# A two-stream transformer layer on one Trainium2 core: the stage between two feed-forward groups rearranged

## The chip, the cores and the metric

The kernel runs on one NeuronCore of a Trainium2 chip. The metric is the device time of one execution in microseconds, lower is better, taken as the median of several runs. The engines, each with its own instruction queue that is worked off in order, are TensorE (PE, matrix products into the banks of PSUM), VectorE (DVE), ScalarE (ACT), GpSimd (POOL) and SyncE (SP, which here issues the DMAs).

## The reference

One encoder layer with the same weights is applied to two request groups: 1024 frames of a new stream and 32 frames of a running one, so 1056 columns in all, with 1024 features and everything in float32.

```python
mod = silu(c) @ w_ada + b_ada
sh1, sc1, g1, sh2, sc2, g2 = split(mod)
h = x * (1 + sc1) + sh1
...                                   # one input projection; three mixers: mLSTM, forgetting attention, gMLP
mix = concat([hm, hf, hg]) @ w_o
x = layer_norm(ALPHA * x + (1 + g1) * mix, ln1_g, ln1_b)
h = x * (1 + sc2) + sh2
y = (silu(h @ w_gate) * (h @ w_up)) @ w_down      # 1024 -> 2816 -> 1024
x = layer_norm(ALPHA * x + (1 + g2) * y, ln2_g, ln2_b)
```

## The kernel before

Features lie on the 128 partitions (KT = 8 tiles of 128 features), columns along the free axis. The 1056 columns are worked as two streams: stream 0 has 512 columns in two cuts of 256, stream 1 has 544 columns in two cuts of 272 (of which the last 32 are the running stream, with its own modulation, so that a cut's work on columns is split into 240 + 32 there). A float32 product is made of three products of rounded halves: `weights` loads a weight tile (`raw`, on SP), rounds it on ACT (`whi`, L102) and takes the rest on DVE (`wlo`, L103); `gemm` issues for each k three matmuls (L114, L115, L116). An activation is split in the same way into a rounded half `ah` and a rest `al`.

The order of the work is this. Input projection and stream 0's mixers; output projection `wo(0)`, norm `ln1(0)`; then the feed-forward part of stream 0 in six groups of its 22 hidden tiles (3, 3, 4, 4, 4, 4), woven by a scheduler with the mixers of stream 1. A group is its `up` calls (gate and up product of one hidden tile, silu by three activations on ACT, L977 to L979, then L980, L981 and L983 on DVE) and a `down` (eight output tiles m, for two cuts each; `sublayer_end` adds a down's result to the residual `z` on DVE, L918, which frees the PSUM bank). The first up of a group is issued before the downs of the group ahead of it.

Before the last group (`g == WOB`, the sixth) stream 1's output projection stands: `wo_mix(1)` reads the mixers' result back from DRAM (16 loads through a tag `tmp` of four buffers, each rounded on ACT, L884, and split on DVE, L885), `wo_res(1)` loads the residual into `z`, `wo(1)` multiplies by w_o, and `ln1(1)` normalises. Then come the last group's ups and downs, and after them the feed-forward part of stream 1.

The norm subtracts a pivot first so that sums of squares keep their precision: `ln_pivot` takes a mean over the first tile (a matmul by `ones8`, L833), copies it (`pv`, ACT, L834) and subtracts it from that tile (L835); for every other tile POOL subtracts it (L915) ahead of the eviction L918. `ln_sum` collects sums (POOL, L845) and squares (ACT L844, DVE L847). `ln_stats` makes the factors r and e of the norm from them (two matmuls, then ACT and DVE, L854 to L866). `ln1` then does for each tile: times r (DVE, L931), plus e (L932, every fourth on POOL), gain and bias (POOL, L935), the rounded half (ACT, L937) and the rest (DVE, L938). `ln1_res` prepares the residual (L947). For stream 0 the pivot that its second norm (`ln2`) needs is subtracted in the downs of the last group.

PSUM has a pool `pg` of three banks, which gate and up products, downs and wo share; a pool `pu` of three further banks for the up products is opened only for stream 1's feed-forward part.

The order of the instructions is set by the Tile framework's scheduler, which places them on each engine by an estimate of the times; `issue_after(x)` holds what is issued in its block behind the instruction x. In the trace a tile carries the name of the phase in which it was made (`wo`, `lna` for the first norm, `up`, `dn`), and z of stream 0 is called `mlstm_z`.

## Time and profile before

| | us |
|---|---|
| median of three runs | 1460.4 (1458.1 to 1462.01) |
| profiled execution, own time | 1461.59 |
| its span, first to last instruction | 1459.8 |
| PE busy | 1396.7 |
| DVE busy | 964.8 |
| ACT busy | 627.2 |
| POOL busy | 283.8 |

The profile is one execution. Its span is the time between the first and the last instruction; 1.8 us lie around it. An engine counts as busy while it executes; "granted clock" is the share of its full clock at which TensorE was allowed to run. A row of a group of instructions names line, engine, operation, written tile and read tiles (buffer numbers left out), shapes and count, then the busy time, the mean duration of one in ns, and the idle time ahead of them with what ended most of it.

### The profile page before, as it was taken

The page shows a single profiled execution, that of the slowest core. Times are in us where ns is not written, and L with a number is a line of the kernel's source. Part 1 is how long each engine was busy: PE and PEld are TensorE (multiplying, and loading weights), DVE is VectorE, ACT ScalarE, POOL GpSimd, SP SyncE. Part 2 cuts the span into 40 slices and gives each one's busy share as a digit, 9 for nine tenths or more (in the row PEclk, how much of TensorE's full clock was granted, in tenths as well). Part 3 has the DMA queues.
Part 4 walks back from the last instruction along what each step waited for, and adds up shares of the span by engine and source line. Part 5 has one row for each costly group of instructions (what it writes and reads, how often), then busy time and mean ns, then how long its engine had stood idle before and what let it go on. Part 6 is the DMA issues. An engine that isn't in the chain of part 4 may idle for free.

```text
span 1459.8 us, 28886 instructions
## 1 busy us (share of the span) xinstructions
PE 1396.7 (96%) x11141; PEld 1345.1 (92%) x11141; DVE 964.8 (66%) x2220; ACT 627.2 (43%) x1365; POOL 283.8 (19%) x335
## 2 busy tenths in 40 slices
PE   7999999999999899999999998998999999999995
PEld 4899988989898799999999998998999999999994
DVE  5558655678698677787877755677648545454676
ACT  3223244534453454555454542334445342424353
POOL 0104100143187300000000000647601000000433
PEclk9999999999999999999999998999999999999997
DMA  9754768563754755444433535321224322222331
GB/s 361 260 194 126 221 199 243 194 197 121 250 188 144 204 166 151 126 125 139 130 111 108 101 94 136 109 86 59 87 73 137 110 87 87 88 88 87 124 108 62
DMA packets 120865, 207.33 MB, mean 142 GB/s; under 512 B 21380, under 2 KB 76300, under 8 KB 120728
## 3 DMA queue, kind: packets, MB, share of 16 engines
q1 hardware_dynamic: 120728, 205.49, 44.8%
q8 instruction: 88, 1.44, 0.4%
q14 instruction: 49, 0.40, 0.1%
HBM read 173.78 MB, written 31.66 MB: 141 GB/s over the span
## 4 chain that ended last, share of the span: by engine, by line
PE 80%; DMA 6%; DVE 6%; POOL 3%; issue 2%; ACT 1%; SPq 1%; DVEq 0%; ACTq 0%; POOLq 0%
PE up_g L115 7%; PE up_g L116 7%; PE up_g L114 7%; PE dn_g L114 4%; PE dn_g L115 4%; PE dn_g L116 4%; PE up_u L116 3%; PE up_u L115 3%; PE up_u L114 3%; PE tm_g L279 3%; PE tm_g L280 3%; PE tm_g L281 3%; PE fox_t L729 2%; PE wo_g L116 2%; PE wo_g L115 2%
## 5 line engine op out<-in xcount | busy, mean ns | idle before, releaser
L114 PE MATMUL up_g<-wo_ah,up_whi 128*128 128x256 f32 (+1 forms) x1056 | 304.1, 289 | 13.2 <-DVE up_sil L980 5.6
L115 PE MATMUL up_g<-wo_al,up_whi 128*128 128x256 f32 (+1 forms) x1056 | 305.3, 289 | 0.1
L116 PE MATMUL up_g<-wo_ah,up_wlo 128*128 128x256 f32 (+1 forms) x1056 | 304.6, 289 | 0.0
L114 PEld LDWEIGHTS up_g<-wo_ah,up_whi 128*128 128x128 f32 x1056 | 201.9, 191 | 16.5 <-DVE up_sil L980 6.0
L115 PEld LDWEIGHTS up_g<-wo_al,up_whi 128*128 128x128 f32 x1056 | 202.1, 191 | 1.4 <-DVE wo_al L938 0.7
L116 PEld LDWEIGHTS up_g<-wo_ah,up_wlo 128*128 128x128 f32 x1056 | 201.7, 191 | 0.7 <-DVE up_wlo L103 0.4
L103 DVE TENSOR_TENSOR up_wlo<-up_raw,up_whi 128x1024 fp32r<-128x1024 f32 x94 | 120.8, 1285 | 68.5 <-ACT up_whi L102 68.2
L102 ACT CAST up_whi<-up_raw 128x1024 fp32r<-128x1024 f32 x94 | 98.5, 1048 | 142.3 <-PE dn_u L115 53.9
L114 PE MATMUL dn_g<-up_acth,dn_whi 128*128 128x256 f32 (+1 forms) x496 | 146.7, 296 | 9.5 <-DVE mlstm_z L918 6.4
L115 PE MATMUL dn_g<-up_actl,dn_whi 128*128 128x256 f32 (+1 forms) x496 | 144.4, 291 | 0.0
L116 PE MATMUL dn_g<-up_acth,dn_wlo 128*128 128x256 f32 (+1 forms) x496 | 143.8, 290 | 0.0
L280 PE MATMUL tm_g<-tm_wlo,start_h1h 128*128 128x256 f32 (+1 forms) x384 | 110.8, 289 | 0.0
L281 PE MATMUL tm_g<-tm_whi,start_h1l 128*128 128x256 f32 (+1 forms) x384 | 110.4, 288 | 0.0
L279 PE MATMUL tm_g<-tm_whi,start_h1h 128*128 128x256 f32 (+1 forms) x384 | 109.8, 287 | 0.2 <-ACT tm_mixs L630 0.2
L114 PE MATMUL fm_g<-start_h1h,fm_whi 128*128 128x256 f32 (+2 forms) x344 | 102.0, 302 | 6.1 <-DVE fm_qkl L364 2.2
L114 PEld LDWEIGHTS dn_g<-up_acth,dn_whi 128*128 128x128 f32 x496 | 96.7, 195 | 11.5 <-DVE mlstm_z L918 7.5
L115 PE MATMUL fm_g<-start_h1l,fm_whi 128*128 128x256 f32 (+2 forms) x344 | 101.8, 296 | 0.2 <-DVE start_h1l L220 0.2
L116 PE MATMUL up_u<-wo_ah,up_wlo 128*128 128x272 f32 x352 | 101.9, 290 | 0.0
L114 PE MATMUL up_u<-wo_ah,up_whi 128*128 128x272 f32 x352 | 101.2, 288 | 0.0
L115 PE MATMUL up_u<-wo_al,up_whi 128*128 128x272 f32 x352 | 101.0, 287 | 0.0
L116 PE MATMUL fm_g<-start_h1h,fm_wlo 128*128 128x256 f32 (+2 forms) x344 | 100.8, 294 | 0.0
L115 PEld LDWEIGHTS dn_g<-up_actl,dn_whi 128*128 128x128 f32 x496 | 96.9, 195 | 0.3
(458 smaller groups left out, 3758.9 us busy)
## 6 DMA issues: line engine op xcount, KB each, us to landing
up_raw<-w_gu SPq DMA_DIRECT2D x94, 512.0 KB
dn_raw<-w_dn SPq DMA_DIRECT2D x30, 512.0 KB
ada_late<-w_ada SPq DMA_DIRECT2D x24, 512.0 KB
wo_raw<-w_o SPq DMA_DIRECT2D x24, 512.0 KB
ada_araw<-w_ada SPq DMA_DIRECT2D x16, 512.0 KB
fm_raw<-w_in_f SPq DMA_DIRECT2D x16, 512.0 KB
tm_raw<-w_in SPq DMA_DIRECT2D x12, 512.0 KB
dn_raw<-w_dn SPq DMA_DIRECT2D x16, 384.0 KB
```

The costliest lines, as they stand in the source:

```text
L102: nc.scalar.copy(hi[:, :w], raw[:, :w])
L103: (eng or nc.vector).tensor_tensor(lo[:, :w], raw[:, :w], f(hi[:, :w]), ALU.subtract)
L114: nc.tensor.matmul(ps, hi, xh(k), start=start and k == 0, stop=False)
L115: nc.tensor.matmul(ps, hi, xl(k), start=False, stop=False)
L116: nc.tensor.matmul(ps, lo, xh(k), start=False, stop=stop and k == n - 1)
L279: nc.tensor.matmul(ps[:, :ncol], xh, hi, start=k == 0, stop=False)
L280: nc.tensor.matmul(ps[:, :ncol], xh, lo, start=False, stop=False)
L281: nc.tensor.matmul(ps[:, :ncol], xl, hi, start=False, stop=k == 7)
L729: nc.tensor.transpose(ps[:, y * P:(y + 1) * P], probs[y][:, b * P:(b + 1) * P], self.ident)
```

## The change

Five things are done. (a) Stream 0's pivot is taken and subtracted in the downs of the fifth group (`g == WOB - 1`) instead of the last group's; the last downs only collect the sums. (b) In `ln1`, for both streams, gain and bias move from POOL to ACT (an activation `Identity` with scale and bias columns). (c) The pool `pu` is opened ahead of stream 1's output projection, so that the last group's ups use six banks. (d) The last group's second up, `up(0, 19)`, is issued ahead of the mix, the mix is issued behind the last residual addition of the fifth group's downs (`lastz`), and each residual tile of stream 1 is loaded inside `wo`. (e) The other two ups are woven with the norm of stream 1 (`up` and `ln1` become generators), and `ln1_res(1)` comes after the last downs.

```diff
-    def wo(self, c, st, cuts, eng):
+    def wo(self, c, st, cuts, eng, res=None):
...
+        if res:
+            self.z[c] = self.t(res, [P, KT, GN[c]], F32, f"z{c}", 1)
+        z = self.z[c]
         ko = self.KORDER
         for m in range(KT):
+            if res:
+                self.load(z[:, m], self.d["xT"][m, :, GO[c]:GO[c] + GN[c]])
             w = self.weights(self.d["w_o"][m], KT, P, eng)
...
         for x, y, i in self.parts(c, a, b):
-            self.nc.vector.scalar_tensor_tensor(z[:, m, x:y], ps[:, x - a:y - a], g[i], z[:, m, x:y],
-                                                ALU.mult, ALU.add)
+            self.lastz = self.nc.vector.scalar_tensor_tensor(z[:, m, x:y], ps[:, x - a:y - a], g[i], z[:, m, x:y],
+                                                             ALU.mult, ALU.add)
...
         for k in range(KT):
+            yield
+            self.phase = f"lna{c}"
             zk = z[:, k, sl]
...
             for x, y, i in self.parts(c, a, b):
-                nc.gpsimd.tensor_scalar(h[:, x - a:y - a], z[:, k, x:y], self.lng[:, k, i:i + 1],
-                                        self.lnb[:, k, i:i + 1], ALU.mult, ALU.add)
+                nc.scalar.activation(h[:, x - a:y - a], z[:, k, x:y], AF.Identity, bias=self.lnb[:, k, i:i + 1],
+                                     scale=self.lng[:, k, i:i + 1])
...
             if g == WOB:
                 s4.close()
                 s3.close()
+                self.pu, self.utag = self.pool("pu", 3, space=PSUM), "gu"
                 pb = self.pb = self.pool("pb", side="right")
+                weave(self.up(0, j0 + 1, act, pa, MM[0]))
                 self.operand(1, pb)
-                self.wo_mix(1, self.KORDER)
-                self.wo_res(1, pb)
+                with tc.issue_after(self.lastz.ins):
+                    self.wo_mix(1, self.KORDER)
                 stb = self.ln_begin(nc.gpsimd)
-                self.wo(1, stb, MM[1], nc.vector)
+                self.wo(1, stb, MM[1], nc.vector, pb)
                 self.operand(1, pb)
-                for a, b in MM[1]:
-                    self.ln1(1, stb, a, b)
+
+                def norm():
+                    for a, b in MM[1]:
+                        yield from self.ln1(1, stb, a, b)
+
+                def fill():
+                    for j in range(j0 + 2, j0 + nj):
+                        yield from self.up(0, j, act, pa, MM[0])
+
+                weave(fill(), norm())
+                continue
...
-            if g == WOB:
-                self.ln1_res(1)
-            if g < last:
+            if g == WOB - 1:
+                st = self.ln_begin(nc.gpsimd, sum=False)
+                self.down(0, g, act, MM[0], st)
+            else:
                 self.down(0, g, act, MM[0])
-        st = self.ln_begin(nc.gpsimd)
+        st.update(pivot=False, sum=True)
         self.down(0, last, act, MM[0], st)
+        self.ln1_res(1)
         s5.close()
         pa = self.pool("pa1")
-        self.pu, self.utag = self.pool("pu", 3, space=PSUM), "gu"
```

What the scheduler makes of it is seen in three places. In the changed kernel line numbers are a few higher: the eviction L918 is L923, the pivot's subtraction L915 is L920, the norm's L931, L932, L935, L937, L938 are L938, L939, L942, L944, L945, the silu's L980, L981, L983 are L990, L991, L993, and `ln1_res`'s L947 is L954.

The first place is DVE at the end of the fifth group's downs, first before (`dn_g` is a down's bank, `wo_tmp` a loaded piece of the mix):

```order
L918 SCALAR_TENSOR_TENSOR mlstm_z_837_4328<-dn_g_12260,start_mod_136,mlstm_z_837_4328 128x256
L885 TENSOR_TENSOR dn_al_2300_12406<-wo_tmp_12408,dn_ah_2298_12404 128x272
L885 TENSOR_TENSOR dn_al_2300_12406<-wo_tmp_12412,dn_ah_2298_12404 128x272
L885 TENSOR_TENSOR dn_al_2300_12406<-wo_tmp_12416,dn_ah_2298_12404 128x272
L885 TENSOR_TENSOR dn_al_2300_12406<-wo_tmp_12420,dn_ah_2298_12404 128x272
L918 SCALAR_TENSOR_TENSOR mlstm_z_837_4328<-dn_g_12280,start_mod_136,mlstm_z_837_4328 128x256
L103 TENSOR_TENSOR wo_wlo_12487<-wo_raw_12484,wo_whi_12486 128x1024
L918 SCALAR_TENSOR_TENSOR mlstm_z_837_4328<-dn_g_12294,start_mod_136,mlstm_z_837_4328 128x256
L918 SCALAR_TENSOR_TENSOR mlstm_z_837_4328<-dn_g_12308,start_mod_136,mlstm_z_837_4328 128x256
L885 TENSOR_TENSOR dn_al_2300_12406<-wo_tmp_12424,dn_ah_2298_12404 128x272
```

The splits L885 of the mix stand between the evictions L918. On the same engine in the changed kernel, from the last eviction of these downs on:

```order
L923 SCALAR_TENSOR_TENSOR mlstm_z_837_4328<-dn_g_12408,start_mod_136,mlstm_z_837_4328 128x256
L885 TENSOR_TENSOR up_al_2319_12564<-wo_tmp_12566,up_ah_2317_12562 128x272
L885 TENSOR_TENSOR up_al_2319_12564<-wo_tmp_12570,up_ah_2317_12562 128x272
L885 TENSOR_TENSOR up_al_2319_12564<-wo_tmp_12574,up_ah_2317_12562 128x272
L885 TENSOR_TENSOR up_al_2319_12564<-wo_tmp_12578,up_ah_2317_12562 128x272
L103 TENSOR_TENSOR wo_wlo_12638<-wo_raw_12635,wo_whi_12637 128x1024
L885 TENSOR_TENSOR up_al_2319_12564<-wo_tmp_12582,up_ah_2317_12562 128x272
L885 TENSOR_TENSOR up_al_2319_12564<-wo_tmp_12586,up_ah_2317_12562 128x272
L885 TENSOR_TENSOR up_al_2319_12564<-wo_tmp_12590,up_ah_2317_12562 128x272
L885 TENSOR_TENSOR up_al_2319_12564<-wo_tmp_12594,up_ah_2317_12562 128x272
L990 TENSOR_TENSOR up_sil_12496<-up_g_12446,up_sil_12496 128x256
```

All sixteen splits now follow the last eviction, and the first silu product of up(0,19), L990, stands behind eight of them, its second (not shown) behind fourteen. The same downs now begin with the pivot: DVE has L835 for both cuts there, and POOL the row below, ahead of the pivot subtractions of stream 1 that stood first before:

```order
L761 MEMSET foxs_q_1826_8499 128x192
L920 TENSOR_TENSOR mlstm_z_837_4328<-mlstm_z_837_4328,up_pv_12152 128x256 x14
L920 TENSOR_TENSOR wo_z_2340_12633<-wo_z_2340_12633,wo_pv_12632 128x272 x7
L845 TENSOR_TENSOR wo_zs_12630<-wo_z_2340_12633 128x272
L920 TENSOR_TENSOR wo_z_2340_12633<-wo_z_2340_12633,wo_pv_12632 128x272 x7
```

The fourteen subtractions of stream 0 do the seven tiles of the first cut, then the seven of the second.

The second place is DVE in `ln1(0)`, at the statistics of the second cut; L364 frees a bank that q/k projections (`fm_g`) hold. Before:

```order
L863 SCALAR_TENSOR_TENSOR lna_tmp_6019<-lna_tmp_6019,wo_pv_5357 128x256
L864 TENSOR_TENSOR lna_tmp_6019<-lna_tmp_6019,wo_pv_5357 128x256
L865 SCALAR_TENSOR_TENSOR wo_pv_5357<-lna_tmp_6019,wo_pv_5357 128x256
L103 TENSOR_TENSOR up_wlo_8707<-up_raw_8704,up_whi_8706 128x1024
L364 SCALAR_TENSOR_TENSOR fm_qkl_6292<-fm_g_6266,start_qsc_127,fm_qkh_6291 128x272
L866 SCALAR_TENSOR_TENSOR wo_qs_5356<-lna_t_6015,wo_pv_5357 128x256
L931 TENSOR_TENSOR mlstm_z_837_4328<-mlstm_z_837_4328,wo_pv_5357 128x256 x8
L364 SCALAR_TENSOR_TENSOR fm_qkl_6333<-fm_g_6307,start_qsc_127,fm_qkh_6332 128x272
```

And in the changed kernel:

```order
L103 TENSOR_TENSOR up_wlo_8707<-up_raw_8704,up_whi_8706 128x1024
L364 SCALAR_TENSOR_TENSOR fm_qkl_6292<-fm_g_6266,start_qsc_127,fm_qkh_6291 128x272
L863 SCALAR_TENSOR_TENSOR lna_tmp_6019<-lna_tmp_6019,wo_pv_5357 128x256
L864 TENSOR_TENSOR lna_tmp_6019<-lna_tmp_6019,wo_pv_5357 128x256
L364 SCALAR_TENSOR_TENSOR fm_qkl_6333<-fm_g_6307,start_qsc_127,fm_qkh_6332 128x272
L865 SCALAR_TENSOR_TENSOR wo_pv_5357<-lna_tmp_6019,wo_pv_5357 128x256
L866 SCALAR_TENSOR_TENSOR wo_qs_5356<-lna_t_6015,wo_pv_5357 128x256
L938 TENSOR_TENSOR mlstm_z_837_4328<-mlstm_z_837_4328,wo_pv_5357 128x256 x8
```

Two of the L364 have moved ahead of the statistics and of the eight products by r.

The third place is DVE in the second half of `ln1(1)`. Before, this half stood ahead of the last downs, with the ups' L980 between its rows:

```order
L938 TENSOR_TENSOR wo_al_2381_13039<-lna_tmp_13123,wo_ah_2379_13037 128x272
L981 TENSOR_TENSOR up_sil_13422<-up_g_13397,up_sil_13422 128x256
L980 TENSOR_TENSOR up_sil_13494<-up_g_13444,up_sil_13494 128x256
L938 TENSOR_TENSOR wo_al_2381_13039<-lna_tmp_13130,wo_ah_2379_13037 128x272
L938 TENSOR_TENSOR wo_al_2381_13039<-lna_tmp_13137,wo_ah_2379_13037 128x272
L981 TENSOR_TENSOR up_sil_13494<-up_g_13469,up_sil_13494 128x256
```

And in the changed kernel, where the last downs have begun (`dn_g` and `dn_u` are their banks, of both pools):

```order
L938 TENSOR_TENSOR wo_z_2340_12633<-wo_z_2340_12633,wo_pv_12632 128x272 x8
L923 SCALAR_TENSOR_TENSOR mlstm_z_837_4328<-dn_g_13666,start_mod_136,mlstm_z_837_4328 128x256
L939 TENSOR_TENSOR wo_z_2340_12633<-wo_z_2340_12633,wo_qs_12631 128x272
L923 SCALAR_TENSOR_TENSOR mlstm_z_837_4328<-dn_g_13609,start_mod_136,mlstm_z_837_4328 128x256
L939 TENSOR_TENSOR wo_z_2340_12633<-wo_z_2340_12633,wo_qs_12631 128x272
L923 SCALAR_TENSOR_TENSOR mlstm_z_837_4328<-dn_u_13642,start_mod_136,mlstm_z_837_4328 128x256
L939 TENSOR_TENSOR wo_z_2340_12633<-wo_z_2340_12633,wo_qs_12631 128x272
```

The half's rows now stand between the evictions L923 of the last downs; its L945 follow later, the first behind ten of the sixteen evictions.

More of the change, by code (lines that the diff above doesn't have):

```diff
@@ L890, in wo_res @@
             self.load(z[:, k], self.d["xT"][k, :, GO[c]:GO[c] + GN[c]])
-    def wo(self, c, st, cuts, eng):
+    def wo(self, c, st, cuts, eng, res=None):
         self.phase = f"wo{c}"
-        nc, z, hh, hl = self.nc, self.z[c], self.hh[c], self.hl[c]
+        nc, hh, hl = self.nc, self.hh[c], self.hl[c]
+        if res:
+            self.z[c] = self.t(res, [P, KT, GN[c]], F32, f"z{c}", 1)
+        z = self.z[c]
         ko = self.KORDER
         for m in range(KT):
+            if res:
+                self.load(z[:, m], self.d["xT"][m, :, GO[c]:GO[c] + GN[c]])
             w = self.weights(self.d["w_o"][m], KT, P, eng)
@@ L975, in up @@
                 ps.append(p)
+                if i == 0:
+                    yield
+                    self.phase = f"up{c}"
             s = self.t(self.p2, [P, 272], F32, "sil", 4)[:, :b - a]
@@ L983, in up @@
             nc.vector.tensor_tensor(al[:, a:b], s, f(ah[:, a:b]), ALU.subtract)
+            yield
+            self.phase = f"up{c}"
     def last_weights(self, dst, units):
@@ L1168, in run @@
         for a, b in MM[0]:
-            self.ln1(0, st, a, b)
+            weave(self.ln1(0, st, a, b))
         for h in range(PRE, 8):
@@ L1186, in run @@
                 s3.close()
+                self.pu, self.utag = self.pool("pu", 3, space=PSUM), "gu"
                 pb = self.pb = self.pool("pb", side="right")
+                weave(self.up(0, j0 + 1, act, pa, MM[0]))
                 self.operand(1, pb)
-                self.wo_mix(1, self.KORDER)
-                self.wo_res(1, pb)
+                with tc.issue_after(self.lastz.ins):
+                    self.wo_mix(1, self.KORDER)
                 stb = self.ln_begin(nc.gpsimd)
-                self.wo(1, stb, MM[1], nc.vector)
+                self.wo(1, stb, MM[1], nc.vector, pb)
                 self.operand(1, pb)
-                for a, b in MM[1]:
-                    self.ln1(1, stb, a, b)
+                def norm():
[6 more added lines that the diff above has]
+                continue
             for j in range(j0 + (g > 0), j0 + nj + (g < last)):
-                self.up(0, j, act, pa, MM[0])
+                weave(self.up(0, j, act, pa, MM[0]))
                 if j < 4:
                     self.ada(20 + j, self.wp, "raw", RAW, self.pg, "g")
-            if g == WOB:
-                self.ln1_res(1)
-            if g < last:
+            if g == WOB - 1:
+                st = self.ln_begin(nc.gpsimd, sum=False)
+                self.down(0, g, act, MM[0], st)
+            else:
                 self.down(0, g, act, MM[0])
-        st = self.ln_begin(nc.gpsimd)
+        st.update(pivot=False, sum=True)
         self.down(0, last, act, MM[0], st)
+        self.ln1_res(1)
         s5.close()
         pa = self.pool("pa1")
-        self.pu, self.utag = self.pool("pu", 3, space=PSUM), "gu"
         act = {}
@@ L1211, in run @@
             for j in range(j0 + (g > 0), j0 + nj + 1):
-                self.up(1, j, act, pa, MM[1])
+                weave(self.up(1, j, act, pa, MM[1]))
             if g == 0:
@@ L1226, in run @@
             for j in range(j0 + 1 + (half and UPF), j0 + nj):
-                self.up(1, j, (act, act2)[half], pa, ((a, b),))
+                weave(self.up(1, j, (act, act2)[half], pa, ((a, b),)))
             if half == 0:
@@ L1230, in run @@
                 for j in range(j0 + 1, j0 + 1 + UPF):
-                    self.up(1, j, act2, pa, (LN[1][1],))
+                    weave(self.up(1, j, act2, pa, (LN[1][1],)))
                 w.update(self.last_weights(((h[:, :n], l[:, :n]), (h[:, n:2 * n], l[:, n:2 * n])), (0, 1)))
```

## Prediction

> **What bounds the kernel now.** I read the page's busy shares first, then its chain, then a table of TensorE (PE) by stage, and last the waits of PE in the stages that showed a loss.
>
> ```profile
> PE 1396.7 (96%) x11141; PEld 1345.1 (92%) x11141; DVE 964.8 (66%) x2220; ACT 627.2 (43%) x1365; POOL 283.8 (19%) x335
> PE 80%; DMA 6%; DVE 6%; POOL 3%; issue 2%; ACT 1%; SPq 1%; DVEq 0%; ACTq 0%; POOLq 0%
> ```
>
> PE is busy for 96% of the span and is 80% of the chain, and the change keeps its matmuls. So the change can only move time in which PE stands still or runs at a lowered clock. Where that is, the stages tell (columns: start and end, length, PE busy and instructions, granted clock, DMA share, GB/s):
>
> ```profile
> 464.00:506.00 42.00, 33.72 (x248) 0.94 0.71 185
> 506.00:850.00 344.00, 343.36 (x2821) 1.00 0.45 129
> 850.00:903.00 53.00, 52.51 (x444) 0.94 0.35 87
> 903.00:914.00 11.00, 6.54 (x33) 0.69 0.93 304
> 914.00:962.00 48.00, 48.00 (x382) 1.00 0.29 102
> 962.00:1033.00 71.00, 60.35 (x445) 0.93 0.19 61
> 1065.00:1460.00 395.00, 377.61 (x2986) 0.98 0.29 97
> ```
>
> Three stages that the change touches lose time. I count for each the idle time plus the part of its length that the clock took. The first norm (464 to 506) loses 8.3 + 42 x 0.06 = 10.8 us. The end of the fifth group's downs (903 to 914) loses 4.5 + 11 x 0.31 = 7.9 us. The second norm with its ups and the pivot (962 to 1033) loses 10.65 + 71 x 0.07 = 15.6 us. Together that is 34 us, the most that these edits can return. The full stages also give the price of a matmul: 343/2821 = 0.122 us for 256 columns, 48/382 = 0.126 us for 272.
>
> The waits of PE in the three, first norm, fifth group, second norm (columns: waited for, us in total, times, longest):
>
> ```profile
> PE up_g L114 <- DVE fm_qkl L364: 4.0, 3, 2.1
> PE up_g L114 <- ACT up_whi L102: 2.9, 1, 2.9
> PE up_g L114 <- ACT wo_ah L937: 0.8, 1, 0.8
> ...
> PE dn_g L114 <- DVE mlstm_z L918: 6.4, 4, 4.5
> ...
> PE up_g L114 <- DVE up_sil L980: 5.6, 2, 2.9
> PE dn_g L114 <- DVE up_sil L980: 3.0, 1, 3.0
> PE dn_g L114 <- DVE mlstm_z L918: 1.9, 3, 0.9
> ```
>
> All are waits for a PSUM bank or a weight whose eviction or split stands in DVE's queue, in order, behind something late. In the second norm that is L938, which waits for ACT, which waits for POOL's affine:
>
> ```profile
> ACT wo_ah L937 <- POOL lna_tmp L935: 18.5, 12, 4.5
> ...
> DVE wo_al L938 <- ACT wo_ah L937: 8.6, 9, 2.0
> ```
>
> **The change, part by part.**
>
> *Affine on ACT (both norms).* One tile needs these operations:
>
> ```profile
> L935 POOL TENSOR_SCALAR lna_tmp<-mlstm_z,wo_lng,wo_lnb 128x256 f32<-128x256 f32 x16 | 14.5, 914 | 0.7 <-DVE mlstm_z L932 0.7
> L1024 ACT ACTIVATE mlstm_z<-mlstm_z,start_colp x16: 585/595/604, 1095.1 to 1120.1; 128x256 f32<-128x256 f32 x16
> L937 ACT CAST wo_ah<-lna_tmp 128x272 fp32r<-128x272 f32 x16 | 6.7, 416 | 18.5 <-POOL lna_tmp L935 18.5
> L931 DVE TENSOR_TENSOR wo_z<-wo_z,wo_pv 128x272 f32<-128x272 f32 x16 | 8.1, 576 | 0.0
> L932 DVE TENSOR_TENSOR wo_z<-wo_z,wo_qs 128x272 f32<-128x272 f32 x12 | 4.9, 462 | 0.0
> L938 DVE TENSOR_TENSOR wo_al<-lna_tmp,wo_ah 128x272 fp32r<-128x272 f32 x16 | 7.1, 447 | 8.6 <-ACT wo_ah L937 8.6
> ```
>
> L1024 is the same form as the new L942 (an activation with two columns as scale and bias), so I price L942 at 0.60 us. ACT then spends 0.60 + 0.42 = 1.0 us on a tile, about POOL's 0.91, but POOL's queue is freed of it: the q/k sums L365, behind whose stores the attention's loads stand on SP, and the residuals no longer stand between the affines. In the first norm the order also puts the wanted L364 ahead of L863. Of the 10.8 us, the L364 waits (4.0) go with the clock drop behind the longest (1.8, below); of up_whi's 2.9, whose load was issued late behind the attention's, and wo_ah's 0.8 I count a third. I take **7 us back**. The ends are 0 (ACT, with 16 x 0.6 = 9.6 us more work in some 35, becomes what PE waits for) and 10.
>
> *Pivot at the fifth group.* The subtraction of the pivot (14 on POOL, L920) moves from the last group's downs to the fifth's, where a down has only the three banks of one pool. There PE must wait for the whole chain at the first tile that wants the pivot, since three tiles (1.45 us each, 12 x 0.122) fill the banks.
>
> ```profile
> L834 ACT COPY lna_pv<-dn_t 128x256 f32<-128x256 f32 x2 | 0.7, 373 | 5.2 <-PE dn_t L833 5.2
> ...
> L915 POOL TENSOR_TENSOR mlstm_z<-mlstm_z,lna_pv 128x256 f32<-128x256 f32 x14 | 12.2, 905 | 4.7 <-ACT lna_pv L834 4.7
> ...
> L918 DVE SCALAR_TENSOR_TENSOR mlstm_z<-dn_g,start_mod,mlstm_z 128x256 f32<-128x256 f32 x21 | 9.8, 476 | 4.2 <-POOL mlstm_z L915 3.1 <-PE dn_g L116 1.1
> ```
>
> Copy 0.37, first subtraction 0.9, eviction 0.48 and the hand-overs (some 0.25) make a first gap of 2.0 us. POOL does the seven first halves before the seven second ones, and DVE's fourth eviction from there waits for the eighth: 0.37 + 8 x 0.9 + 0.48 = 8.1 us after the pivot. PE has by then had the gap and two or three tiles, 4.9 to 6.3 us, so a second gap of 1.8 to 3.2, of which I take 2.4. Does a gap of 2.0 us cost clock? These are the rows nearest to it:
>
> ```profile
> 464.38 0.29 PE L116 MATMUL fm_g<-start_h1h,fm_wlo 128*128 128x272 f32 x1
> 466.81 0.58 PE L114 MATMUL up_g<-wo_ah,up_whi 128*128 128x256 f32 x1 [2.14 <-DVE fm_qkl L364]
> 467.19 0.42 PE L115 MATMUL up_g<-wo_al,up_whi 128*128 128x256 f32 x1
> ...
> 1025.04 0.38 PE L114 MATMUL dn_g<-up_acth,dn_whi 128*128 128x256 f32 x1 [0.65 <-DVE mlstm_z L918]
> 1025.26 0.28 PE L115 MATMUL dn_g<-up_actl,dn_whi 128*128 128x256 f32 x1
> ...
> 460.00:480.00 20.00, 15.93 (x110) 14.81 (x108) 18.69 (x35) 8.30 (x19) 18.47 (x24) 0.91 0.47 146
> ```
>
> After 2.14 us the matmuls took 0.42 instead of 0.28 us, after 0.65 they did not; one drop cost 20 x 0.09 = 1.8 us. 2.0 is nearer to 2.14, so I add 1.8. [...] Pivot: **6.2 us lost** (3 to 8), while the 1.9 us of waits at its old place are part of the 15.6.
>
> *Mix split behind the residual.* The 16 loads of the mix go through four buffers; each buffer is freed by its split L885. Before, L885 stood in front of evictions and held them up:
>
> ```profile
> 905.56 1.53 ACT L884 CAST dn_ah<-wo_tmp 128x272 fp32r<-128x272 f32 x4 [9.52 <-DMA wo_tmp<-start_dmix]
> 909.81 1.17 ACT L884 CAST dn_ah<-wo_tmp 128x272 fp32r<-128x272 f32 x3 [1.78 <-DMA wo_tmp<-start_dmix]
> 917.18 1.59 ACT L884 CAST dn_ah<-wo_tmp 128x272 fp32r<-128x272 f32 x4 [2.80 <-DMA wo_tmp<-start_dmix]
> ...
> 906.01 1.56 DVE L885 TENSOR_TENSOR dn_al<-wo_tmp,dn_ah 128x272 fp32r<-128x272 f32 x4 [6.18 <-ACT dn_ah L884]
> 907.48 0.48 DVE L918 SCALAR_TENSOR_TENSOR mlstm_z<-dn_g,start_mod,mlstm_z 128x256 f32<-128x256 f32 x1
> ...
> L885 DVE TENSOR_TENSOR dn_al<-wo_tmp,dn_ah x16: 431/442/444, 895.5 to 919.2; 128x272 fp32r<-128x272 f32 x16
> ```
>
> Now no eviction waits for them, so the **7.9 us come back**. But the first four splits, done at 895 before, come after the last residual too, and three rounds of four loads follow. Between the ACT rows a round took 4.25 us, and 7.4 with weight loads beside it, 5.8 on the mean. The last split is then 1.6 + 3 x 5.8 = 19 us after the last residual. The filler up(0,19) gives 96 x 0.122 = 11.7 us, and PE needs the last split some 50 matmuls into the output projection, at 18 us; the third round's first split is wanted after 12 us and comes at about 13.5. Behind the splits wait the evictions L990 of the second filler cut, and with them a bank; they end at the same time. I take **2 us lost**, with ends 0 (rounds of 4.25) and 7.8 (rounds of 7.4: 24 - 18 = 6, and 1.8 of clock). The residual's eight loads now stand on SP ahead of the last twelve mix loads; they issue while those wait for buffers, so I cost them at nothing; without that cover they would lengthen one round.
>
> *Fillers and six banks in the second norm.* The ups no longer share three banks, the first two of their L990 stand ahead of every L945, and the second half's norm runs beside the last downs, which don't need it. 15.6 us were lost; I leave 3: DVE has 16 evictions x 0.48, 8 x 0.58 + 6 x 0.46 + 8 x 0.45 for the half norm, and about five weight splits of 1.3, some 25 us and the silu's part beside 16 x 1.45 = 23 us of downs, so the first up of the second stream may wait a little. **12.6 us back**, ends 8 and 15. The moved residual affine (L954) is POOL's, which is empty there, and its reader is the next group of downs, far behind.
>
> The mixers between 506 and 850 keep their order but for small shifts: 0, within 3 either way. From 1065 on, nothing is moved.
>
> Sum: 7 + 7.9 - 6.2 - 2 + 12.6 = 19.3 us. The profiled execution took 1461.6, so 1442.3; it stands 1.2 above the median of the three runs, so **1441 us**. A change under 0.3%, 4.4 us, can't be told from none here.
>
> **Rivals.**
> 1. *The mix wait comes back at the output projection.* For it: only four buffers, SP in order, and 7.4 us for a round beside weight loads, which wo now issues as well. Against: the 4.25 round. Price 7.8 us instead of 2 and a third wo weight late by some 2: 1449.
> 2. *ACT becomes the pacer of the first norm.* For it: 9.6 us more for an engine that also casts every weight there. Against: it had 8.3 us of work in 20. The 7 us don't come: 1448.
> 3. *The second norm still stalls.* DVE's in-order queue puts a silu or a bank behind an L945, as it did behind L938. 5 us back instead of 12.6: 1449.
> 4. *Slower: evictions of the last downs and the second half's norm lock step.* In DVE's new order the evictions L923 alternate with L939 and L945. If each tile's eviction waits for a whole norm tile, 0.58 + 0.46 + 0.6 + 0.3 (second piece of the affine) + 0.42 + 0.45 = 2.8 us, eight times, with a clock drop of 1.8 on most: 8 x 2.8 + 7 x 1.8 = 35 us lost where 15.6 were lost: 1441 + 32 = 1473. The kernel gets slower by more than 0.3% once this stage loses over 3 + 20 + 4.4 = 27 us. Against: six banks, and the first L945 of that half stands behind ten evictions.
>
> **How the numbers follow.** Forecast 0.55 (1433 to 1447); rivals 1, 2 and 3: 0.15, 0.12 and 0.08; two of them at once, which ends within 0.3%, 0.06; rival 4 0.04. Faster 0.89, same 0.06, slower 0.05. The good ends (10, 7.9, 4.4 lost for the pivot, 0 for the mix, 15) with the mixers' 3 make 31.5 us, 1429; the bad ones short of the double cases stop near 1454. So 1429 to 1454.
>
> **What would show it.** Right: no PE wait for L364 over 1 us near 464; two PE gaps of about 2 us at the fifth group's downs behind POOL's L920; no L885 ahead of an L923 there, and PE within 3 us of full between the last residual and the projection; no PE wait for L990 over 1 us in the second norm, and PE busy for all but 3 us until the second stream's first ups. Wrong: a gap of 5 us or more before wo's second cut, ACT rows as the releaser of PE in the first norm, or a row of equal gaps through the last downs.

## The result, and the profile after

| | us |
|---|---|
| changed kernel, median of four runs | 1436.7 (1431.9 to 1437.7) |
| kernel before, median of four runs beside it | 1461.0 (1458.1 to 1462.0) |
| ratio, 95% interval | 0.9826 (0.9809 to 0.9844) |
| profiled execution of the changed kernel, own time | 1436.1 |
| its span | 1434.3 |

The change saves 24.2 us of 1461.0. In a later comparison it gave 0.9826 again (0.980 to 0.985). 1441 was forecast, so the direction and the range were right; by terms it was less right than the sum shows.

The page of the changed kernel, busy shares and chain:

```profile
PE 1385.6 (97%) x11141; PEld 1336.3 (93%) x11141; DVE 960.7 (67%) x2220; ACT 641.3 (45%) x1405; POOL 254.3 (18%) x295
PE 82%; DMA 7%; DVE 6%; ACT 1%; issue 1%; SPq 1%; POOL 1%; DVEq 0%; ACTq 0%; POOLq 0%
```

PE has the same 11141 matmuls. The 40 activations that ACT gained are the 40 instructions that POOL lost. PE by stage in the changed kernel (columns: start and end, length, PE busy and instructions, granted clock, DMA share, GB/s):

```profile
456.00:500.00 44.00, 40.25 (x308) 0.92 0.72 208
500.00:835.00 335.00, 334.25 (x2742) 1.00 0.46 132
835.00:886.00 51.00, 51.00 (x446) 0.97 0.26 81
886.00:893.00 7.00, 4.60 (x32) 1.00 0.91 31
893.00:1014.00 121.00, 121.00 (x989) 1.00 0.36 119
```

From 893 us on, through the rest of the fifth group's downs, the projection, the second norm and the last downs, PE is busy for 121.0 of 121 us at full clock; this stretch held the stalls at 903 and from 979 to 1033 before. What is left is the pivot's gap (886 to 893) and, unexpected, a loss in the first norm. The waits of PE behind the two, first norm (456 to 500), then from 883 to 1014:

```profile
PE up_g L114 <- ACT lna_tmp L942: 3.3, 1, 3.3
PE up_g L115 <- DVE wo_al L945: 0.4, 1, 0.4
...
PE dn_g L114 <- DVE mlstm_z L923: 2.4, 2, 1.8
```

To compare executions I cut each at marks on PE that all kernels share and take start to start:

| us | before | changed |
|---|---|---|
| up to the first matmul of wo(0) | 387.1 | 391.5 |
| wo(0) | 50.6 | 49.9 |
| first norm, up to stream 0's first downs | 104.3 | 99.3 |
| mixers of stream 1, up to the fifth downs | 335.3 | 334.5 |
| fifth downs to the last down's end | 163.2 | 138.1 |
| up to stream 1's first downs | 47.7 | 48.9 |
| the rest of the matmuls | 356.1 | 355.6 |

25.1 us come from the stretch from the fifth downs to the end of the last ones, 5.0 from the first norm. The marks do not cut quite the same matmuls in both kernels. In the changed one seven matmuls of the mixers come ahead of stream 0's first downs instead of behind them, some 0.8 us, and nine of stream 1's first up come behind the last down instead of ahead of it, 9 x 0.122 = 1.1 us. For the same matmuls, then, the first norm gained 5.8 us and the stretch from the fifth downs on 24.0, and the mixers and the stretch after the last downs are as long as before.

Two things scatter from execution to execution. The first row is the same code in both: over the fourteen profiles of this study it lies between 385.8 and 392.8, so 4.4 us of it are the scatter of one execution. And behind the mixers' small matmuls, at the start of the fifth downs, matmuls at half clock (granted 0.50 from 877.30 to 879.65 us before and from 875.20 to 875.84 in the changed kernel, 0.21 us from start to start instead of 0.12) cost 2.5 us in the kernel before and 0.4 in the changed one; over the fourteen profiles this lies between 0.1 and 2.5, so the difference of 2.1 is not the change's.

### The profile page after: what moved, and what is told of

Its sections match the earlier page's. It is cut to its first block, busy times and chain, and to the rows that moved or that the text cites. A ratio compares the mean times of both kernels' runs of the same rounds, so it can differ in the third digit from the quotient of the medians.

```text
span 1434.3 us, 28877 instructions
## 1 busy us (share of the span) xinstructions
PE 1385.6 (97%) x11141; PEld 1336.3 (93%) x11141; DVE 960.7 (67%) x2220; ACT 641.3 (45%) x1405; POOL 254.3 (18%) x295
## 4 chain that ended last, share of the span: by engine, by line
PE 82%; DMA 7%; DVE 6%; ACT 1%; issue 1%; SPq 1%; POOL 1%; DVEq 0%; ACTq 0%; POOLq 0%
PE up_g L115 8%; PE up_g L116 8%; PE up_g L114 8%; PE dn_g L114 4%; PE dn_g L115 4%; PE dn_g L116 4%; PE up_u L116 3%; PE up_u L115 3%; PE up_u L114 3%; PE tm_g L279 2%; PE tm_g L280 2%; PE tm_g L281 2%; PE fox_t L729 2%; PE wo_g L114 2%; PE wo_g L115 2%; PE wo_g L116 2%
## 5 line engine op out<-in xcount | busy, mean ns | idle before, releaser
L114 PE MATMUL up_g<-wo_ah,up_whi 128*128 128x256 f32 (+1 forms) x1008 | 288.8, 287 | 3.4 <-ACT lna_tmp L942 3.3
L115 PE MATMUL up_g<-wo_al,up_whi 128*128 128x256 f32 (+1 forms) x1008 | 290.4, 288 | 0.4 <-DVE wo_al L945 0.4
L116 PE MATMUL up_g<-wo_ah,up_wlo 128*128 128x256 f32 (+1 forms) x1008 | 289.4, 287 | 0.0
L114 PEld LDWEIGHTS up_g<-wo_ah,up_whi 128*128 128x128 f32 x1008 | 191.4, 190 | 4.9 <-ACT wo_ah L944 3.5
L114 PE MATMUL dn_g<-up_acth,dn_whi 128*128 128x256 f32 (+1 forms) x464 | 133.8, 289 | 2.4 <-DVE mlstm_z L923 2.4
L115 PE MATMUL dn_g<-up_actl,dn_whi 128*128 128x256 f32 (+1 forms) x464 | 132.3, 286 | 0.0
L116 PE MATMUL dn_g<-up_acth,dn_wlo 128*128 128x256 f32 (+1 forms) x464 | 132.1, 285 | 0.0
L116 PE MATMUL up_u<-wo_ah,up_wlo 128*128 128x272 f32 (+1 forms) x400 | 115.4, 289 | 0.0
L114 PE MATMUL up_u<-wo_ah,up_whi 128*128 128x272 f32 (+1 forms) x400 | 114.9, 287 | 0.0
L115 PE MATMUL up_u<-wo_al,up_whi 128*128 128x272 f32 (+1 forms) x400 | 114.5, 286 | 0.0
```

What stands on the lines that cost most here:

```text
L114: nc.tensor.matmul(ps, hi, xh(k), start=start and k == 0, stop=False)
L115: nc.tensor.matmul(ps, hi, xl(k), start=False, stop=False)
L116: nc.tensor.matmul(ps, lo, xh(k), start=False, stop=stop and k == n - 1)
```

## The experiments

Each edit is against the changed kernel unless it says otherwise. Every ratio is to the kernel before that was run beside it; the changed kernel stands at 0.9826. The intervals reach 0.2 to 0.4% to either side of a ratio, so that the stretches above, which are finer but come from one execution each, are given beside them.

**The mix queued freely.** Does the fifth group's stall come back when the splits are not held behind the residual?

```diff
-                with tc.issue_after(self.lastz.ins):
-                    self.wo_mix(1, self.KORDER)
+                self.wo_mix(1, self.KORDER)
```

> The changed kernel, but the mix splits L885 are not held behind the last residual: DVE's order then has them between the evictions L923 of the fifth group's downs again, the second round's four behind only four evictions. If holding them back is what returned the 4.5 us of idle time and the clock drop there (the theory of the prediction, 7.9 us), PE again waits 4 to 7 us for an L923 in these downs, and the time is 1440 to 1445. If the earlier pivot or the filler up(0,19) is what removed the wait (rival), the time stays at 1436 to 1438 and PE shows no wait over 1 us besides the pivot's two.

Measured 1442.6 us, ratio 0.987 (0.984 to 0.990). From the fifth downs to the last ones PE took 146.0 us instead of 138.1. The waits of PE there, and DVE's rows around the longest one:

```profile
PE dn_g L114 <- DVE mlstm_z L923: 7.1, 3, 4.7
...
890.99 0.88 DVE L923 SCALAR_TENSOR_TENSOR mlstm_z<-dn_g,start_mod,mlstm_z 128x256 f32<-128x256 f32 x2 [1.61 <-PE dn_g L116]
898.06 0.80 DVE L885 TENSOR_TENSOR up_al<-wo_tmp,up_ah 128x272 fp32r<-128x272 f32 x2 [6.18 <-ACT up_ah L884]
898.77 0.48 DVE L923 SCALAR_TENSOR_TENSOR mlstm_z<-dn_g,start_mod,mlstm_z 128x256 f32<-128x256 f32 x1
```

DVE sat 6.18 us before a split whose rounded half was late, with the next eviction behind it, and PE waited 4.7 us for that eviction's bank: the stall of before. Of the 7.9 us 1.5 are a lowered clock behind the pivot, which comes and goes (last section); the order behind the residual is worth the other 6.

**No filler over the mix.** The up of hidden tile 19 goes back to the other two:

```diff
-                weave(self.up(0, j0 + 1, act, pa, MM[0]))
...
-                    for j in range(j0 + 2, j0 + nj):
+                    for j in range(j0 + 1, j0 + nj):
```

> The changed kernel, but up(0,19) comes with the other fillers beside the norm, not ahead of the output projection. In the changed kernel's trace the mix took 16.2 us from the last residual to the last split, and the projection's first tile has about 6 us of matmuls of its own. If the filler is the cover, PE idles some 10 us at the projection's start and pays one clock drop: 1446 to 1449. If the splits only look late because DVE has the filler's silu among them (rival), the mix takes 9 to 10 us and the loss is 3 to 5: 1440 to 1442.

Measured 1442.3 us, ratio 0.987 (0.983 to 0.990); the stretch took 142.4, so 4.3 us more. PE's waits from 885 to 1014:

```profile
PE dn_g L114 <- DVE mlstm_z L923: 2.4, 2, 1.7
PE wo_g L114 <- ACT dn_ah L884: 1.2, 2, 0.9
PE wo_g L115 <- DVE dn_al L885: 0.9, 1, 0.9
PE wo_t L833 <- DVE wo_z L923: 0.6, 1, 0.6
```

The first row is the pivot's and stands in the changed kernel as well. Without the filler PE meets the mix, but only in short waits at the start of the projection. The filler is worth about 4 us, not the length of the mix. The loss is of the rival's size, but not for the rival's reason: the mix did not shrink to 9 or 10 us, its last split still began 14.2 us after the last residual (16.2 with the filler). The interval of the ratio alone touches that of the changed kernel; the stretch and these waits tell them apart.

**Three banks.** The pool `pu` opens after the last downs again:

```diff
-                self.pu, self.utag = self.pool("pu", 3, space=PSUM), "gu"
...
         pa = self.pool("pa1")
+        self.pu, self.utag = self.pool("pu", 3, space=PSUM), "gu"
```

> The changed kernel with the second PSUM pool opened only for the second stream, so that the last group's ups and downs share three banks as before. Theory: the norm stage's 15.6 us came back through banks and fillers together, and with three banks PE again waits for L990 and L923 that stand behind the norm's rows: some 6 to 12 us of waits, 1443 to 1449. Rival: the affine on ScalarE and the second half's place beside the downs suffice, 1437 to 1439.

Measured 1444.3 us, ratio 0.988 (0.985 to 0.992). The stretch took 147.7, 9.6 us more; 1.9 of these are 15 matmuls of stream 1's first up that here come ahead of the last down (the next stretch is 1.9 shorter), and 1.2 the lowered clock at the start, so the banks are worth some 6.5. The waits from 880 to 1020 are back on evictions and the silu:

```profile
PE dn_g L114 <- DVE mlstm_z L923: 5.1, 4, 1.8
PE dn_g L114 <- DVE up_sil L991: 1.1, 1, 1.1
```

**The affine back on POOL in one norm.** First in the second norm, then, in a kernel of its own, in the first one (`c == 0`):

```diff
+                if c == 1:
+                    nc.gpsimd.tensor_scalar(h[:, x - a:y - a], z[:, k, x:y], self.lng[:, k, i:i + 1],
+                                            self.lnb[:, k, i:i + 1], ALU.mult, ALU.add)
+                else:
+                    nc.scalar.activation(...)
```

> The changed kernel with gain and bias of the second stream's norm back on GpSimd, everything else as changed. Theory: with six banks and the half norm beside the downs PE no longer waits for the affine's engine, except where the second stream's first ups want the last rows: GpSimd needs 24 affines of about 0.85 us, 20 us in all beside the sums and the residuals, so the second half comes 5 to 8 us late and the time is 1439 to 1445. Rival A: the place of the affine is the whole gain, 1449 to 1453. Rival B: it is fully hidden, 1435 to 1438.

> The changed kernel with gain and bias of the first stream's norm (464 to 506 us before) back on GpSimd; its order there is again that of the kernel before. Theory (prediction: 7 us, the changed profile: 5.7 between the first output projection and the first downs): the early gain goes, 1442 to 1445. Rival: the early difference is only the scatter of the loads in the first 390 us, and the time stays within 2 us of 1437.

Second norm: 1444.0 us, ratio 0.988 (0.984 to 0.991). The stretch took 141.4 (3.3 more, of which 1.3 is a lowered clock behind the pivot), and the one up to stream 1's first downs 52.8 instead of 48.9. PE's waits there (880 to 1035):

```profile
PE dn_g L114 <- DVE mlstm_z L923: 2.4, 2, 1.7
PE dn_g L114 <- ACT up_acth L996: 1.5, 1, 1.5
PE up_g L114 <- ACT wo_ah L948: 1.4, 1, 1.4
```

The norm ends later on POOL, and it is stream 1's first up that waits for it. First norm: 1444.8 us, ratio 0.986 (0.984 to 0.988). The first norm's stretch is at 104.2 us again, as before the change, with the old waits (456 to 510):

```profile
PE up_g L114 <- DVE fm_qkl L364: 4.0, 3, 2.1
PE up_g L114 <- ACT up_whi L102: 2.1, 1, 2.1
PE up_g L114 <- ACT wo_ah L948: 0.8, 1, 0.8
```

So the early gain is this one instruction's engine. The eight profiles with the affine on ACT and nothing further changed in this norm have 99.3 to 101.2 us there, the two with it on POOL 104.2 and 104.3. The changed kernel's profile is the best of the eight, so 3 to 5 us is the fairer figure.

**The affine alone, on the kernel before.** The opposite test: before.py's `ln1` with the activation and nothing else of the change.

> The kernel before with one part of the change: gain and bias on ScalarE in both norms, nothing else. Theory: the first norm's part comes whole, 5 to 6 us; in the second norm, with three banks and no work beside it, the shorter chain takes away the GpSimd waits but not the queue of DVE: 3 to 8 of its 18 us. Time 1447 to 1453. Rival: without banks and fillers the second norm stalls as before, 1455.

Measured 1451.3 us, ratio 0.991 (0.988 to 0.993), so 13.6 us of the 24. The first norm's stretch gives 3.6 us, the one from the fifth downs on 9.0 (154.2 instead of 163.2), of which some 2.5 are the lowered clock at its start. The fifth group's stall stays, and a wait for the silu too (885 to 1035):

```profile
PE dn_g L114 <- DVE mlstm_z L918: 8.1, 5, 6.0
PE up_g L114 <- DVE up_sil L980: 4.2, 3, 2.6
```

**The pivot at the last downs.** Now that those have six banks, its place of before might be free:

```diff
-            if g == WOB - 1:
-                st = self.ln_begin(nc.gpsimd, sum=False)
-                self.down(0, g, act, MM[0], st)
-            else:
-                self.down(0, g, act, MM[0])
-        st.update(pivot=False, sum=True)
+            self.down(0, g, act, MM[0])
+        st = self.ln_begin(nc.gpsimd)
```

> The changed kernel with the pivot back in the last group's downs, which now have six banks. Theory: the pivot cost 2.0 + 0.8 us of gaps at the fifth group because three banks fill in 4.3 us; six banks hold 8.5 us of downs, as long as the first eight subtractions take, so at the last downs it costs under 1 us and the time falls by some 2 us to 1434 or 1435. Rival: there DVE also has the second half's norm between the evictions, and GpSimd the sums; gaps of 3 to 6 us come up in the last downs, 1438 to 1441.

Measured 1440.3 us, ratio 0.983 (0.980 to 0.986), which can't be told from the changed kernel; the stretch took 141.0 instead of 138.1, but some 1.7 of the 2.9 are the lowered clock at its start. The gap is as long there (880 to 1020), and DVE's rows ahead of it show why:

```profile
PE dn_u L114 <- DVE mlstm_z L923: 2.3, 3, 1.9
...
997.38 5.08 DVE L938 TENSOR_TENSOR wo_z<-wo_z,wo_pv 128x272 f32<-128x272 f32 x8
1002.38 0.95 DVE L835 TENSOR_TENSOR mlstm_z<-mlstm_z,lna_pv 128x256 f32<-128x256 f32 x1
1003.25 0.96 DVE L939 TENSOR_TENSOR wo_z<-wo_z,wo_qs 128x272 f32<-128x272 f32 x1
1004.13 0.47 DVE L923 SCALAR_TENSOR_TENSOR mlstm_z<-dn_u,start_mod,mlstm_z 128x256 f32<-128x256 f32 x1
```

Six banks do not hide it, because the first eviction behind the pivot stands in DVE's queue behind the eight products of stream 1's norm. That is the rival's reason, though the gap is shorter than its 3 to 6 us.

**The first norm's new gap.** In the changed kernel PE waits 3.3 us there for the affine itself. ACT is not the cause: it stood idle for 1.20 us until DVE's sum L939 came. POOL, DVE and ACT ahead of PE's wait, and below them two steps of the chain of waits:

```profile
453.62 5.92 POOL L954 TENSOR_SCALAR mlstm_z<-mlstm_z,start_colp 128x256 f32<-128x256 f32 x4 [1.36 <-ACT lna_tmp L942]
...
460.32 0.50 DVE L364 SCALAR_TENSOR_TENSOR fm_qkl<-fm_g,start_qsc,fm_qkh 128x272 fp32r<-128x272 f32 x1 [1.13 <-POOL fm_qkr L365]
464.14 0.50 DVE L364 SCALAR_TENSOR_TENSOR fm_qkl<-fm_g,start_qsc,fm_qkh 128x272 fp32r<-128x272 f32 x1 [2.24 <-POOL mlstm_z L954]
...
474.71 1.58 ACT L942 ACTIVATE lna_tmp<-mlstm_z,wo_lnb,wo_lng 128x256 f32<-128x256 f32 x3 [1.20 <-DVE mlstm_z L939]
...
459.54 0.75 POOL fm_qkr L365
...
460.88 3.15 DMA start_dql<-fm_qkl
```

With the affine gone from POOL, its residual product L954 is free to run as soon as each tile of the norm is read. Four of them stand in front of the q/k sum L365, for which DVE's first L364 here waits. The second wait, which its row puts down to an L954, ends in the chain with a store of `fm_qkl` that SP issued only behind these POOL rows and that took 3.15 us. The second half's factors stand behind that L364 on DVE. So L954 is held behind the last q/k sum:

```diff
-                nc.gpsimd.tensor_copy(self.qks[:, h, :], kr[:, n - NS:n])
+                self.lastq = nc.gpsimd.tensor_copy(self.qks[:, h, :], kr[:, n - NS:n])
...
-        self.ln1_res(0)
+        with tc.issue_after(self.lastq.ins):
+            self.ln1_res(0)
```

> The changed kernel with the first stream's residual affines (L954 on GpSimd) held behind the last q/k sum L365. In the changed profile PE waits 3.3 us for the norm (gap of 4.5 at 474 us and 2.0 of lowered clock), and DVE had waited 1.1 and 2.2 us before for a buffer that an L365 behind these L954 held. If that queue is the cause, the gap shrinks to 1 us or less and the time falls by 4 to 6 us: 1431 to 1433. If the late load of a weight behind the stores (up_raw landing at 472) is the cause by itself (rival), the gap stays, 1435 to 1438.

Measured 1432.4 us, ratio 0.979 (0.976 to 0.982). The first norm's stretch is 96.8 us instead of 99.3, and PE's wait shorter:

```profile
PE up_g L114 <- ACT lna_tmp L942: 1.9, 1, 1.9
PE up_g L115 <- DVE wo_al L945: 0.6, 1, 0.6
```

DVE's waits ahead of L364 are down to one of 0.82 us, for the store. The mechanism holds, but the gap is not gone: 1.9 us were left where 1 or less was expected. Since the gain over the changed kernel is small, both were run again:

> The changed kernel once more, beside the two that follow, to have all three on one chip: 0.982 to 0.984 of the kernel before, and in the profile the pivot's gaps of 2.0 and 0.8 us and the gap of the first norm again (theory); the lowered clock behind the first of them in some executions and not in others, since the same gap had it in three of seven profiles.

> The changed kernel with the first residual affines held behind the last q/k sum, again, with more rounds: if the 2.5 to 4 us that its profile showed less between the first output projection and the first downs are the queue's (theory), the ratio to the kernel before is 0.979 to 0.981 again, 0.002 to 0.003 under the changed kernel's 0.9826; if the first run's time was scatter of the stages before (rival), it is 0.982 to 0.984.

The changed kernel gave 1437.5 us, ratio 0.983 (0.980 to 0.985), with a first norm of 100.9 us; the one with L954 late 1432.9 us, 0.980 (0.977 to 0.982), with 97.4. The intervals touch, and the two were run on different chips, each beside the kernel before. Yet both ratios are 0.003 to 0.004 lower, 4 to 6 us, and both stretches, 96.8 and 97.4, lie below all eight of 99.3 to 101.2. This is the fastest version of this study.

**The norm's products and sums interleaved.** The rest of that gap is eight products by r on DVE ahead of the first sum; here every product waits for the sum of the tile ahead of it:

```diff
-            nc.vector.tensor_tensor(zk, zk, r, ALU.mult)
-            (nc.gpsimd if k % 4 == 1 else nc.vector).tensor_tensor(zk, zk, e, ALU.add)
+            with self.tc.issue_after(prev.ins) if prev else ExitStack():
+                mul = nc.vector.tensor_tensor(zk, zk, r, ALU.mult)
+            add = (nc.gpsimd if k % 4 == 1 else nc.vector).tensor_tensor(zk, zk, e, ALU.add)
+            prev = mul if k % 4 == 1 else add
```

> The changed kernel with the first residual affines held behind the last q/k sum (as in the run on that) and, in both norms, each tile's product by r held behind the tile before it, so that DVE does not do eight products in one block. In the changed profile this block (8 in 4.0 us) stands between the statistics and the first tile that the ups want, and PE waits there. Theory: the first tile comes 3 us earlier, PE's gap in the first norm and the lowered clock behind it go, 3 to 5 us less than with the residuals alone: 0.975 to 0.977 of the kernel before. Rival: the q/k evictions that DVE has among these rows decide, not the block; as with the residuals alone, 0.979.

Measured 1438.1 us, ratio 0.983 (0.981 to 0.985): no gain over the changed kernel, and 4 to 6 us lost against L954 late alone. The long gap of the norm is gone, and a new one stands in the attention behind it. PE's waits (456 to 505), a row each of POOL and ACT, and a step of the chain of waits:

```profile
PE fox_t L729 <- DVE fox_p L715: 2.8, 1, 2.8
PE up_g L114 <- DVE up_sil L993: 2.1, 2, 1.7
PE up_g L115 <- DVE wo_al L948: 1.6, 2, 0.9
...
471.08 9.28 POOL L957 TENSOR_SCALAR mlstm_z<-mlstm_z,start_colp 128x256 f32<-128x256 f32 x12
481.10 1.58 ACT L945 ACTIVATE lna_tmp<-mlstm_z,wo_lnb,wo_lng 128x256 f32<-128x256 f32 x3 [2.54 <-POOL mlstm_z L941]
...
484.59 4.09 DMA mlstm_mb<-start_dM
```

Twelve residual products (L957 here) now run in one block on POOL. The norm's own sum on POOL, L941, stands behind them, and the last three affines wait for it. A load of the mixers that follows a POOL instruction there is issued late too, and DVE waits for that load with the attention's L715 in its queue. The theory that the order of products and sums was all that kept PE waiting fell.

**The pivot's mean in a bank of the pool `pg`.** On the kernel just described, the matmul of `ln_pivot` at the fifth group writes to the downs' pool instead of its own:

```diff
-        ps = self.t(self.pt, [P, 512], F32, "t")
+        ps = self.t(self.pg, [P, 512], F32, "g") if st.get("early") else self.t(self.pt, [P, 512], F32, "t")
```

> As the run before it, and the fifth group's pivot is taken in a bank of the downs' own pool instead of the pool that it shares with the mixers' last transposes, so it need not stand behind these in PE's order and comes after the first down tile instead of the fifth. Theory: the chain of copy and first subtraction then runs beside the second and third tile, and the 2.0 us gap shrinks to two short waits for the first evictions, 1 us or less each: 1 to 2.5 us less than the run before. Rival: the pivot takes one of three banks and PE stops for each of the two evictions as long as before, no difference.

Measured 1440.6 us, ratio 0.985 (0.983 to 0.988), against 0.983 (0.981 to 0.985) of the kernel it was put on: no gain, and the stretch from the fifth downs to the last ones is as long (133.8 and 134.2). PE waits for the same eviction, now ahead of the mean (875 to 1014):

```profile
PE dn_g L833 <- DVE mlstm_z L923: 1.9, 2, 1.6
```

## Why the prediction came out right, and where its terms did not

**Bound and mechanism: right.** PE's matmuls are unchanged and the time is PE's idle and slow time: in the stretch from the fifth downs to the end of the last ones, what the spacings of PE's starts have over their usual length (0.119 us for 256 columns, 0.125 for 272; the prediction's 0.122 for 256 is the mean of a stage that also holds the mixers' smaller and larger matmuls) comes to 28.2 us before and 4.2 after. The 24.0 between them are the whole difference for the same matmuls.

**First norm: 7 us forecast, 5.0 measured** (104.3 to 99.3, or 5.8 for the same matmuls; 3.4 in the second profile of the changed kernel, 4.9 by undoing it alone). The waits for L364 are gone from PE, as forecast, but they moved onto DVE, behind POOL's L954, and come back as the 3.3 us wait for L942. With that an ACT row is PE's releaser in the first norm, which the prediction had named as a sign of being wrong; but ACT was itself waiting for DVE, so rival 2 is not what happened. The step that failed is "the residuals no longer stand between the affines": true, but they stood between the q/k sums instead. The cost of L942 was right, 0.597 against 0.60:

```profile
L942 ACT ACTIVATE lna_tmp<-mlstm_z,wo_lnb,wo_lng x16: 583/597/605, 452.9 to 480.7; 128x256 f32<-128x256 f32 x16
```

**Pivot: 6.2 us forecast, 2.8 measured.** This is below the 3 to 8 that the prediction allowed. The first gap was 2.13 us between starts, 2.0 lost, as worked out, though the eviction that ended it stood behind the two L835 on DVE and not behind POOL. The hand-overs, which the forecast put at some 0.25 us in all, were 0.04 from PE to ACT, 0.08 from ACT to POOL, 0.08 from POOL to DVE and 0.06 from DVE to PE at the pivot of the profile before (1017 to 1025 us). The second was 0.93 instead of 2.4:

```profile
887.37 11.13 POOL L920 TENSOR_TENSOR mlstm_z<-mlstm_z,up_pv 128x256 f32<-128x256 f32 x14 [63.45 <-ACT up_pv L834]
892.28 0.48 DVE L923 SCALAR_TENSOR_TENSOR mlstm_z<-dn_g,start_mod,mlstm_z 128x256 f32<-128x256 f32 x1 [2.57 <-PE dn_g L116]
893.39 0.48 DVE L923 SCALAR_TENSOR_TENSOR mlstm_z<-dn_g,start_mod,mlstm_z 128x256 f32<-128x256 f32 x1 [0.62 <-POOL mlstm_z L920]
```

The step that failed is the eviction that PE is made to wait for. The fourth one did wait for POOL's eighth subtraction, as forecast. But PE went on at 892.82 already, with the bank that the third one freed, and the third had waited for nothing but PE's own last matmul of its tile. That POOL's subtractions took 0.80 us each and not 0.9 only brings the fourth eviction forward.

The clock drop of 1.8 did not come in this execution. Moving the pivot gained nothing that the time shows: at the last downs the longest gap is of the same size.

**Mix: 2 us forecast, 0 measured; the 7.9 us behind it right.** The last eviction and the splits on DVE:

```profile
907.05 0.48 DVE L923 SCALAR_TENSOR_TENSOR mlstm_z<-dn_g,start_mod,mlstm_z 128x256 f32<-128x256 f32 x1 [2.08 <-PE dn_g L116]
907.45 1.49 DVE L885 TENSOR_TENSOR up_al<-wo_tmp,up_ah 128x272 fp32r<-128x272 f32 x4
...
923.25 0.44 DVE L885 TENSOR_TENSOR up_al<-wo_tmp,up_ah 128x272 fp32r<-128x272 f32 x1
```

They took 16.2 us from the last residual, where 19 were forecast, and PE waited for none. What the order held back are DVE's splits alone: ACT had rounded the first four pieces at 887.6 us already. Rival 1 did not occur.

**Second norm: 12.6 us forecast, some 17.5 measured**, above the 15 that the prediction allowed. The loss before had been read from windows, busy time and mean clock, as 15.6; counted from start to start it was 17.2, or 18.7 if spacings under the usual one are not set against those over it (three waits of 3.0, 2.9 and 3.2, three runs of 1.5 at half clock, the first at a granted 0.50 from 982.3 to 985.6 us, the rest in smaller ones). The changed kernel leaves 0 to 1.0, not 3. So two errors added, both towards too little. Undone one at a time, the mix (7.9), the banks (9.6), the filler (4.3), the affine here (7.2 with the stage behind it) and the pivot's place (2.9) cost 31.9 us, and some 26 once the moved matmuls and the scatter of the clock are taken off. That is more than the stretch gained (25.1, or 21.9 in the same terms), and the affine alone brought 7.3 of them in the second norm: the parts guard some of the same time, and no share of that belongs to one alone. Rivals 3 and 4 did not occur.

That the sum was only 4 us off is in part luck. The stretch from the fifth downs on was forecast to give 12.3 us and gave 24.0 for the same matmuls: some 5 more in the second norm, 3.4 in the pivot, 2 in the mix, and 2.1 that no term had, the lowered clock behind the mixers' small matmuls at its start (2.5 us in the execution before, 0.4 in this one); these add up to it within 1 us. Against it stand, in the same pair of executions, 1 to 2 us too much in the first norm and the 4.4 of the start.

## What to carry to other kernels

An instruction that moves to another engine frees more than its own time: look at what the engine it leaves will now run earlier, and in front of whom. Work that nobody needs soon (here a residual product, which held up the q/k sums behind it in POOL's queue for 5.9 us) was better held back by name than left to run when its input was ready (96.8 us for the first norm's stretch instead of 99.3). Count a stage's loss from start to start of the bounding engine's instructions, since busy time with a mean clock took 15.6 us for what was 17.2 at the least; and count the matmuls between two marks, since an order that moves a few across a mark looks like a gain (25.1 us for 24.0).

## What the runs showed of the hardware

**The clock after a short gap.** The same gap of 2.13 us behind the pivot stands in nine profiles. In six of them the matmuls after it ran at full clock, as here in the changed kernel (start, duration; granted clock 1.00 from 889.06 to 892.10 us):

```profile
889.06 0.39 PE L114 MATMUL dn_g<-up_acth,dn_whi 128*128 128x256 f32 x1 [1.75 <-DVE mlstm_z L923]
889.29 0.28 PE L115 MATMUL dn_g<-up_actl,dn_whi 128*128 128x256 f32 x1
```

In three (the mix queued freely, the affine back on POOL in either norm) the matmuls after it were slowed, 0.21 us from start to start instead of 0.12: 16 of them with the mix queued freely, which cost 1.5 us, and 15 with the second norm's affine on POOL, which cost 1.3 (granted clock 0.64 from 887.60 to 892.20 us); here with the first norm's affine on POOL:

```profile
897.29 0.58 PE L114 MATMUL dn_g<-up_acth,dn_whi 128*128 128x256 f32 x1 [1.75 <-DVE mlstm_z L923]
897.66 0.41 PE L115 MATMUL dn_g<-up_actl,dn_whi 128*128 128x256 f32 x1
```

So the forecast's rule, a drop behind every gap of about 2 us, was wrong, and so was the price: in these nine profiles it is a third of 1.4 us. The row that the forecast took for the nearest was also a longer gap: its 2.14 us are idle time, 1.75 here.

**POOL beside DVE.** A residual product L954 took 1.48 us (5.92/4) while DVE worked through the norm, busy for 5.57 of the 5.92 us, and 0.62 (8.03/13) where it was held behind the last q/k sum and DVE was busy for 2.64 of the 6.00 us from 478 to 484:

```profile
476.38 8.03 POOL L954 TENSOR_SCALAR mlstm_z<-mlstm_z,start_colp 128x256 f32<-128x256 f32 x13
```

At 1.48 us each, four of them held up the q/k sums for 5.9 us. Whether DVE's work made the difference was not shown: no run here took it away alone.
